# A hybrid encoder trunk on one core: the first norm's gain moved to the evictions, the later norms and the attention's last tiles moved into neighbouring products, and attention scores as two float32r products

## Chip, core and metric

The kernel runs on one core of a Trainium2 chip. The metric is device time in microseconds (us) of one execution, lower is better. Engines are named as in the profile: PE is TensorE's matrix products, PEld its weight loads, DVE is VectorE, ACT is ScalarE, POOL is GpSimd, SP is SyncE (which here only queues transfers).

## What is computed

Two layers over 512 tokens of width 1024, in float32. Cut to what matters here:

```python
def rms_norm(x, g):
    return x * lax.rsqrt(jnp.mean(x * x, axis=-1, keepdims=True) + EPS) * g

def fox_mix(h, w_in, fgate_b, q_g, k_g, w_out):       # 16 heads of 64
    q, k, v, fz = jnp.split(h @ w_in, [hd, 2 * hd, 3 * hd], axis=-1)
    q, k = rms_norm(q per head, q_g), rms_norm(k per head, k_g)
    c = jnp.cumsum(jax.nn.log_sigmoid(fz + fgate_b), axis=1)
    for each block i of 128 queries, keys :hi up to its end:
        logits = q[lo:hi] @ k[:hi].T * 64 ** -0.5 + c[lo:hi, None] - c[None, :hi]
        probs = softmax(where(causal, logits, -inf)); out = probs @ v[:hi]
    return concat(outs) @ w_out

def reference(x, ...):
    x = x + even_mix(rms_norm(x, g0))    # convolution and gated linear attention
    x = x + peer_ffn(rms_norm(x, g1))    # 16384 experts, 128 chosen per token
    x = x + fox_mix(rms_norm(x, g2))
    return x + peer_ffn(rms_norm(x, g3))
```

## The kernel before

One program runs four stages one after the other: `mix_even`, `peer(0)`, `mix_odd` and `peer(1)`. The residual `x` stays on the chip as four blocks of 128 tokens, `xb[0..3]`. Tile, the framework, gives each engine one fixed order of instructions (worked out when the program is built) and places the waits; the code sets it through the order in which it is written, through pools of buffers, and through `issue_after`.

Products of full precision are made of float32r pieces. `split` (L50 to 52) makes a high half on ACT (L51) and the rest on DVE or POOL (L52); `mm3` (L76 to 80) does high x high (L78), low x high (L79) and high x low (L80).

A norm (`rms_body`, L96) goes block by block. `scale` is a Square on ACT with the row's sum (L105), two small steps on DVE and POOL (L106, L107), and the scaling by the row's factor and the gain row `grow` on DVE (L108). `flip` transposes the block in two sets of four 128x128 squares on PE (L115) and evicts each set as `hhi` on ACT (L117) and `hlo` on DVE (L118). `grow` is the gain spread over 128 partitions by a load of 512 KB on SP (L86). `hhi` and `hlo` feed the projection behind the norm. A norm starts when the stage before it is through with `x`, and PE has the transposes to do and little else.

`mix_odd` is the attention. For each pair of heads, `project` makes 128 columns of q or k; `normalise` sums the squares on PE (L622), takes the root with Ln and Exp on ACT (L224, L225) and writes each head's 64 rows, scaled, to `qa` or `ka` (L628), whose two further rows are the cumulated gate and ones (queued on SP, L630). `logits` makes one score block (L640, float32, 66 rows deep) and adds the mask (L641); the softmax is L643 to L648; `flip` transposes the probabilities (L659), evicted to `PT` by ACT (L662) or DVE (L664); `values` multiplies them with v (L672). There are 64 units (head, block of queries); transposes of a unit follow three units after its scores. Units of one head pair lie between the projections of the next. The output projection `out_proj` (L195) follows when all units are done; it adds to `x` (L200).

`peer` begins with its norm, then runs expert steps `u_step` (L843, `pu` in the rows, 384 columns of blocks 1 to 3) and query projections; POOL gathers expert rows for block 0 by indirect transfers (L862, L873). It ends with `v_sweep`s (L1028), one per block, and the additions to `x` (L1062).

## Time and profile before

| | us |
|---|---|
| three runs, median (lowest to highest) | 3106.2 (3104.6 to 3106.36) |
| the profiled execution, its own time | 3103.41 |
| its span in the trace | 3101.6 |
| PE busy | 3058.7 (99%) |
| DVE, ACT, POOL busy | 2401.2, 1384.7, 1096.6 |
| `mix_even` / `peer(0)` / `mix_odd` / `peer(1)`, PE's first instruction of each at | 10 / 271 / 1530 / 1838 |

Busy time is an average over stages with different limits. PE's products are pipelined: a row's length exceeds the step from one to the next, so steps are read from the chain of waits or from the starts. A float32 product shows as two records. In the timeline, an entry in brackets is the idle time before the instruction and what ended it.

### The profile page before, as it was taken

How to read it: one execution, taken by the hardware profiler on the slowest of the kernel's cores; microseconds unless marked ns; L12 is line 12 of the kernel's file. 1: busy time of each engine (PE TensorE's matmuls, PEld its weight loads, DVE VectorE, ACT ScalarE, POOL GpSimd, SP SyncE). 2: the span in 40 equal slices, each digit the busy share in tenths (PEclk: the TensorE clock that was granted, in tenths of full speed). 3: DMA queues.
4: the chain of work that ended last, by engine and by line, in shares of the span. 5: the costliest groups of instructions: out<-in, count | busy, mean ns of one | idle time of the engine just before them, and what ended most of it. 6: DMA issues, size and time to landing. Idle time of an engine off the chain costs nothing.

```text
span 3101.6 us, 45719 instructions
## 1 busy us (share of the span) xinstructions
PE 3058.7 (99%) x15932; PEld 2684.7 (87%) x15932; DVE 2401.2 (77%) x4936; ACT 1384.7 (45%) x2224; POOL 1096.6 (35%) x800
## 2 busy tenths in 40 slices
PE   8999999999999999999999999999999999999999
PEld 6668999999999888888776679999999998888887
DVE  6764998888886888888645638898888867888886
ACT  4444334666664333333344523336666653333332
POOL 1220122976674222222100000227866752222220
PEclk9999999999999999999999999999999999999999
DMA  4113444999999899999421124448999998999996
GB/s 158 55 35 116 137 144 159 353 363 336 343 320 329 298 356 363 366 363 370 172 82 42 42 78 142 137 142 311 380 336 345 336 326 278 356 369 357 376 363 219
DMA packets 334201, 787.15 MB, mean 254 GB/s; under 512 B 26745, under 2 KB 181770, under 8 KB 327826
## 3 DMA queue, kind: packets, MB, share of 16 engines
q1 hardware_dynamic: 260242, 515.76, 47.5%
q0 software_dynamic: 73728, 268.47, 24.5%
q8 instruction: 125, 2.05, 0.3%
q14 instruction: 106, 0.87, 0.1%
HBM read 687.59 MB, written 96.47 MB: 253 GB/s over the span
## 4 chain that ended last, share of the span: by engine, by line
PE 92%; DVE 3%; issue 2%; DMA 1%; POOL 1%; ACT 1%; DVEq 0%; POOLq 0%; ACTq 0%
PE acc L1033 32%; PE pu L79 11%; PE pu L80 11%; PE pu L78 11%; PE bank L78 6%; PE bank L80 5%; PE bank L79 5%; PE bank L912 5%; PE pc L285 1%; PE po L672 1%; PE bank L640 1%; PE bank L936 1%; DMA gr<-in_uN_dram,ids 1%; DVE wlo L52 1%; PE bank L659 1%
## 5 line engine op out<-in xcount | busy, mean ns | idle before, releaser
L51 ACT ACTIVATE whi<-raw 128x1024 fp32r<-128x1024 f32 x604 | 639.8, 1060 | 1500.6 <-issue 584.8
L52 DVE TENSOR_TENSOR wlo<-raw,whi 128x1024 fp32r<-128x1024 f32 x565 | 692.4, 1226 | 339.1 <-ACT whi L51 309.7
L78 PE MATMUL pu<-hhi,whi 128*128 128x384 f32 x2048 | 699.1, 341 | 1.2 <-ACT hhi L117 1.2
L80 PE MATMUL pu<-hhi,wlo 128*128 128x384 f32 x2048 | 688.2, 336 | 2.6 <-DVE wlo L52 2.6
L79 PE MATMUL pu<-hlo,whi 128*128 128x384 f32 x2048 | 686.8, 335 | 0.0
L873 POOL DMA_INDIRECT gr<-in_vF_dram,ids x256 | 277.0, 1082 | 720.8 <-DVE x L875 696.2
L1033 PE MATMUL acc<-wlo,wh 128*128 128x512 f32 x1536 | 439.2, 389 | 0.0
L1033 PE MATMUL acc<-whi,wh 128*128 128x512 f32 x1536 | 439.1, 389 | 0.0
L862 POOL DMA_INDIRECT gr<-in_uN_dram,ids x256 | 349.2, 1364 | 252.4 <-DVE dots L864 157.3
L1033 PE MATMUL acc<-whi,wl 128*128 128x512 f32 x1536 | 436.8, 389 | 0.0
L78 PEld LDWEIGHTS pu<-hhi,whi 128*128 128x128 f32 x2048 | 386.2, 189 | 3.0 <-ACT hhi L117 1.7
L80 PEld LDWEIGHTS pu<-hhi,wlo 128*128 128x128 f32 x2048 | 385.6, 188 | 3.4 <-DVE wlo L52 3.2
L79 PEld LDWEIGHTS pu<-hlo,whi 128*128 128x128 f32 x2048 | 386.2, 189 | 1.7 <-DVE hlo L118 0.3
L1033 PEld LDWEIGHTS acc<-whi,wl 128*128 128x128 f32 x1536 | 288.4, 188 | 59.9
L1033 PEld LDWEIGHTS acc<-wlo,wh 128*128 128x128 f32 x1536 | 288.4, 188 | 59.7
L1033 PEld LDWEIGHTS acc<-whi,wh 128*128 128x128 f32 x1536 | 288.4, 188 | 59.5
L875 DVE SCALAR_TENSOR_TENSOR x<-gr,dots,x 128x1024 f32<-128x1024 f32 x256 | 327.2, 1278 | 0.0
L864 DVE CUSTOM_DVE_ANT_0 gr<-gr,h 128x1024 f32<-128x1024 f32 x256 | 308.6, 1225 | 20.9 <-DMA gr<-in_uN_dram,ids 20.7
L902 POOL TENSOR_SCALAR a<-cst,sT 128x128 f32<-128x128 f32 x192 | 316.3, 1648 | 15.2 <-PE bank L912 5.6
L52 POOL TENSOR_TENSOR wlo<-raw,whi 128x1024 fp32r<-128x1024 f32 x39 | 98.1, 2515 | 396.1 <-ACT whi L51 388.1
L899 DVE TENSOR_TENSOR a<-cst,sT 128x512 f32<-128x512 f32 x192 | 133.4, 695 | 126.2 <-PE bank L912 114.8
L78 PE MATMUL bank<-hhi,whi 128*128 128x512 f32 x512 | 211.5, 414 | 3.5 <-DVE hlo L118 2.7
(244 smaller groups left out, 4095.7 us busy)
## 6 DMA issues: line engine op xcount, KB each, us to landing
raw<-in_uT_dram SPq DMA_DIRECT2D x256, 512.0 KB
raw<-in_vF_dram SPq DMA_DIRECT2D x256, 512.0 KB
G<-big SPq DMA_DIRECT2D x48, 1024.0 KB
gc<-G SPq DMA_DIRECT2D x32, 1536.0 KB
aside<-xact SPq DMA_DIRECT2D x208, 192.0 KB
at<-aside SPq DMA_DIRECT2D x104, 384.0 KB
raw<-in_w_in_dram SPq DMA_DIRECT2D x32, 512.0 KB
raw<-in_wq_dram SPq DMA_DIRECT2D x32, 512.0 KB
```

Source lines behind the costliest of these rows:

```text
L51: first = self.nc.scalar.activation(hi, raw, AF.Copy)
L52: self.last_lo = (eng or self.nc.vector).tensor_tensor(lo, raw, hi.bitcast(F32), op=ALU.subtract)
L78: mm(out, lh, rh, start=first, stop=False)
L79: mm(out, lh, rl, start=False, stop=False)
L80: return mm(out, ll, rh, start=False, stop=last)
L862: nc.gpsimd.indirect_dma_start(out=r, out_offset=None, in_=uN, in_offset=bass.IndirectOffsetOnAxis(ap=ids[:, s:s + 1], axis=0))
L864: return lambda: nc.vector.tensor_tensor_reduce(r, r, h0, 1.0, 0.0, ALU.mult, ALU.add, accum_out=dots[:, s:s + 1])
L873: nc.gpsimd.indirect_dma_start(out=r, out_offset=None, in_=vF, in_offset=bass.IndirectOffsetOnAxis(ap=ids[:, s:s + 1], axis=0))
L875: return lambda: nc.vector.scalar_tensor_tensor(self.x0, r, dots[:, s:s + 1], self.x0, op0=ALU.mult, op1=ALU.add)
L902: (nc.vector if t else nc.gpsimd).tensor_scalar(a1[:, t], self.iota, e1[:, t:t + 1], gate[:, t:t + 1], op0=ALU.is_equal, op1=ALU.mult)
L912: nc.tensor.matmul(p[:, t], a2[:, t], a1[:, t], start=True, stop=True)
L1033: nc.tensor.matmul(acc[b][c], wt[:, s], vt[:, c], start=(n == 0 and wt is wh and vt is vh), stop=(n == NE1 - 1 and wt is wl))
```

## The change

1. **First norm** (`first_norm`). `scale` leaves the gain out; transposes go by columns, all four blocks of a column set into one bank, and the gain, now one number per partition (`gc0`), is applied by the eviction (`scale=` on ACT, and in the subtraction on DVE). The loads of x1 to x3 and of four weights stand at the head of SP's queue; the gain row of the next norm comes later. The conversion of `steps` moves to POOL, into `peer(0)`.
2. **Norms** (`norm`, in place of `rms_h`). Square writes its squares into the buffer that the scaled rows take. `scale` and `flip` can be called one by one. PEER 0's norm is called as before, with two buffers. The attention's norm is called in PEER 0's last `v_sweep`s, and its first value products (`start`) lie between its transposes. The norm of PEER 1 is called in the second half of `out_proj`. Block 0, the last, comes behind the first expert step.
3. **Scores**. `normalise` makes x scaled once for both heads (`xn`), splits it, and copies each high half to the other 64 partitions by transfers that POOL issues. Tile `a` holds (q: high, low; k: high, high), tile `b` (q: high; k: low) and four rows for the gate's sums and ones. A score is two float32r products, over `a` and `b`, of at least 256 columns. k has one pair of tiles now, q two. The gate's sums go through HBM (`cD`).
4. **Attention's end**. The last units run between the weights of `out_proj`'s first half. `values` is called before `flip`; `PT` has one buffer.

```diff
-        def scale(b):
...
             rs = self.np.tile([P, 1], F32, name="rs", bufs=NB)
-            xs[b] = h0 if b == 0 and h0 is not None else rp.tile([P, D], F32, name="xs", bufs=2)
-            sq = rp.tile([P, D], F32, name="sq")
-            self.last_sq = nc.scalar.activation(sq, self.xb[b], AF.Square, accum_out=ss)
+            xs[b] = rp.tile([P, D], F32, name="xs", bufs=blocks) if dst is None else dst
+            self.last_sq = nc.scalar.activation(xs[b], self.xb[b], AF.Square, accum_out=ss)
             nc.vector.tensor_scalar(ss, ss, 1.0 / D, EPS, op0=ALU.mult, op1=ALU.add)
             nc.gpsimd.tensor_tensor(rs, ss, self.mhalf, op=ALU.pow)
-            nc.vector.scalar_tensor_tensor(xs[b], self.xb[b], rs, self.grow, op0=ALU.mult, op1=ALU.mult)
...
     def mix_even(self):
         nc, tc, A = self.nc, self.tc, self.A
         hT = self.new_hT()
+        gc = self.np.tile([P, KD], F32, name="gc0")
+        nc.sync.dma_start(gc, A["gain0"])
+        for b in range(1, NB):
+            nc.sync.dma_start(self.xb[b], A["x"][b * P:(b + 1) * P])
+
+        self.early = [self.raw(A["w_in0"][i]) for i in (0, 4, 3, 7)]
         with tc.tile_pool(name="m0c", bufs=1) as sc:
-            self.rms_h(0, hT)
...
+            for k in range(KD):
+                p = self.bank([P, NB, P])
+                for b in range(NB):
+                    nc.tensor.transpose(p[:, b], xs[b][:, k * P:(k + 1) * P], self.ident)
+                p = p.rearrange("p b t -> p (b t)")
+                nc.scalar.activation(hT[0][:, k], p, AF.Copy, scale=gc[:, k:k + 1])
+                nc.vector.scalar_tensor_tensor(hT[1][:, k], p, gc[:, k:k + 1], hT[0][:, k].bitcast(F32),
+                                               op0=ALU.mult, op1=ALU.subtract)
```

The scores:

```diff
+                parts = [sb.tile([16, T], F32R, name=x, tag="t2", bufs=self.t2) for x in ("chi", "clo")]
+                self.split(pc, *parts)
+                for n, part in enumerate(parts):
+                    nc.sync.dma_start(cD[:, n], part.bitcast(F32))
...
             aug, PT, po = {}, {}, {}
-            qk = [[sp.tile([66, 2, T], F32, name=f"{x}a{j}") for j in range(2)] for x in "qk"]
+
+
+            qk = [[(sp.tile([P, 2, T], F32R, name=f"{x}a{j}"), sp.tile([68, 2, T], F32R, name=f"{x}b{j}"))
+                   for j in range(2 - w)] for w, x in enumerate("qk")]
...
+                for _, b in qk[w]:
+                    nc.gpsimd.dma_start(b[66 - 2 * w:68 - 2 * w], A["ends"][w])
...
-                a = qk[w][hp % 2]
+                a, b = qk[w][hp % len(qk[w])]
+                x = sb.tile([P, T], F32, name="xn", tag="t2", bufs=self.t2)
+                nc.vector.scalar_tensor_tensor(x, p, qkg[:, w:w + 1], rs, op0=ALU.mult, op1=ALU.mult)
                 for h in range(2):
-                    s = slice(h * 64, (h + 1) * 64)
-                    nc.vector.scalar_tensor_tensor(a[0:64, h], p[s], qkg[s, w:w + 1], rs[s],
-                                                   op0=ALU.mult, op1=ALU.mult)
-                    nc.sync.dma_start(a[64 + w:65 + w, h], cT[2 * hp + h:2 * hp + h + 1, w])
-                aug[hp, w] = a
+                    s, o = [slice(j * 64, (j + 1) * 64) for j in (h, 1 - h)]
+                    hi = a[s, h]
+                    nc.scalar.activation(hi, x[s], AF.Copy)
+                    lo, copy = (b[0:64, h], a[o, h]) if w else (a[o, h], b[0:64, h])
+                    nc.vector.tensor_tensor(lo, x[s], hi.bitcast(F32), op=ALU.subtract)
+                    nc.gpsimd.dma_start(copy, hi.bitcast(F32))
+                nc.gpsimd.dma_start(b[64 + 2 * w:66 + 2 * w], cD[2 * hp:2 * hp + 2].rearrange("h n t -> n h t"))
+                aug[hp, w] = a, b
...
                 pS = self.bank()
-                nc.tensor.matmul(pS[:, 0:n], qa[:, h, i * P:n], ka[:, h, 0:n], start=True, stop=False)
+                for j in range(2):
+                    nc.tensor.matmul(pS[:, 0:max(n, 2 * P)], aug[hp, 0][j][:, h, i * P:n],
+                                     aug[hp, 1][j][:, h, 0:max(n, 2 * P)], start=(j == 0), stop=False)
...
                 if i == 0:
-                    PT[hp, h] = sb.tile([P, NB, T], F32, name="PT")
+                    PT[hp, h] = sb.tile([P, NB, T], F32, name="PT", bufs=1)
...
+                if n - AHEAD - 1 >= 0 and units[n - AHEAD - 1][2] == NB - 1:
+                    values(*units[n - AHEAD - 1][:2])
                 if 0 <= n - AHEAD < len(units):
                     flip(units[n - AHEAD])
-                if n - AHEAD - 1 >= 0 and units[n - AHEAD - 1][2] == NB - 1:
-                    values(*units[n - AHEAD - 1][:2])
...
-            for _ in range(8 + AHEAD + 1):
-                unit()
-            self.out_proj(A["w_out1"], self.rows(oT))
+            self.hT = self.new_hT()
+            self.out_proj(A["w_out1"], self.rows(oT), i=3, hT=self.hT, between=lambda: [unit() for _ in range(4)],
+                          middle=lambda: pool.__exit__(None, None, None))
```

The projection's end, PEER's beginning and the last sweeps (`run` puts each call behind the one before in PE's order):

```diff
+        def ends(sweeps, acc):
+            run = self.chain()
+
+            def finish(b):
+                add(1, b, acc[b])
+                if b:
+                    nc.sync.dma_start(self.kept[b - 1], self.xb[b])
+                    scale(b)
+
+            for b in DB:
+                for f in sweeps:
+                    run(f, b)
+                finish(b)
+            for n, f in enumerate(sweeps):
+                if n == 0:
+                    run(flip, 1, hT)
+                    run(flip, 2, hT)
+                if n == 2:
+                    run(flip, 3, hT)
+                run(f, 0)
+            finish(0)
+            self.run = run
...
+            if L == 0:
+                nc.sync.dma_start(self.stf, A["steps"])
+                for w in range(2):
+                    nc.gpsimd.tensor_copy(self.steps[:, w], self.stf[:, w, :, None].to_broadcast([P, TOPK, TOPK]))
+                hT = self.new_hT()
+                self.keep()
+                scale, flip, close = self.norm(1, 2)
+                scale(1)
+                for b in DB:
+                    scale((b + 1) % NB, None if b < NB - 1 else h0)
+                    flip(b, hT)
+                    nc.sync.dma_start(self.kept[b - 1], self.xb[b])
+                run = lambda f, *args: f(*args)
...
+            def last():
+                run(flip, 0, hT)
+                close()
+                self.close_x()
...
+        run(lambda: u_step(0)[1])
+        nu = 1
+        last()
...
+        if L == 0:
+            hN, (scale, put, _), start = self.odd_begin()
+            with tc.issue_after(self.last_lo.ins):
+                scale(0)
+        run = self.chain()
         for b in range(nd):
-            v_sweep(tail, b)
+            run(v_sweep, tail, b)
             for c in range(2):
                 xa = self.xb[DB[b]][:, c * 512:(c + 1) * 512]
-                nc.vector.tensor_tensor(xa, xa, acc[b][c], op=ALU.add)
+                with tc.issue_after(self.last_xs.ins) if L == 0 else nullcontext():
+                    nc.vector.tensor_tensor(xa, xa, acc[b][c], op=ALU.add)
+            if L == 0:
+                scale(DB[b])
+                if b == 1:
+                    run(put, 0, hN, True)
+        if L == 0:
+            for b in DB:
+                run(put, b, hN, True)
+                run(start, b - 1)
+            run(start, NB - 1)
```

**SP's queue at the start.** `x` are the blocks of the input, `cst` constants, `stf` the steps, `raw` a weight as loaded. The queue before:

```order
1 L1076 DMA x_72<-in_x_dram 128x1024
2 L1077 DMA cst<-in_consts_dram 128x128
3 L1087 DMA stf<-in_steps_dram 128x32
4 L86 DMA grow<-in_gains_dram 128x1024
5 L1092 DMA x<-in_x_dram 128x1024 x3
6 L1093 DMA cst<-in_consts_dram 128x1024
7 L241 DMA cw<-in_conv_w_dram 128x124
8 L243 DMA ch<-in_conv_c_dram 128x12
```

SP's queue at the same place with the change:

```order
1 L1226 DMA x_72<-in_x_dram 128x1024
2 L1227 DMA cst<-in_consts_dram 128x128
3 L295 DMA gc_87<-in_gain_dram 128x8
4 L297 DMA x<-in_x_dram 128x1024 x3
5 L59 DMA raw<-in_w_in_dram 128x1024 x4
6 L301 DMA cst<-in_consts_dram 128x1024
7 L332 DMA cw<-in_conv_w_dram 128x124
8 L334 DMA ch<-in_conv_c_dram 128x12
9 L336 DMA gw_202<-in_gate_w_dram 17x256
10 L338 DMA glg<-in_gla_g_dram 128x1
11 L215 DMA wgr<-in_w_glr_dram 128x128
12 L95 DMA grow<-in_gains_dram 128x1024
```

The gain row went from ahead of x1 to x3 to the end of what is shown; four weights and the small `gc` came forward.

**PE and POOL in the attention**, where a unit of 512 columns and the sum of squares of the next pair stand. `idb` and `nmask` are the mask, `pr` the probabilities, `sq` the squares. PE there before:

```order
5722 L659 MATMUL bank<-cst,pr 128x128 x4
5723 L640 MATMUL bank<-ka_14268,qa_14266 128x512
5724 L641 LDWEIGHTS idb
5725 L641 MATMUL bank<-nmask,idb 128x128
5726 L672 MATMUL po<-PT,v 64x512
5727 L672 MATMUL po<-PT,v 64x384
5728 L672 MATMUL po<-PT,v 64x256
5729 L672 MATMUL po<-PT,v 64x128
5730 L659 MATMUL bank<-cst,pr 128x128
5731 L622 MATMUL bank<-sq,cst 128x512
```

PE at the same place now; the score is two rows, and the values kept their place behind it:

```order
5755 L776 MATMUL bank<-cst,pr 128x128 x4
5756 L756 MATMUL bank<-ka_14265,qa_14263 128x512
5757 L756 MATMUL bank<-kb_14266,qb_14264 128x512
5758 L758 LDWEIGHTS idb
5759 L758 MATMUL bank<-nmask,idb 128x128
5760 L789 MATMUL po<-PT,v 64x512
5761 L789 MATMUL po<-PT,v 64x384
5762 L789 MATMUL po<-PT,v 64x256
5763 L789 MATMUL po<-PT,v 64x128
5764 L776 MATMUL bank<-cst,pr 128x128
5765 L733 MATMUL bank<-sq,cst 128x512
5766 L87 MATMUL bank<-hhi,whi 128x512
```

POOL now, from its first three loads of the rows of sums on (before, POOL has no instruction among the attention's units):

```order
224 L746 DMA qb_14262<-cD 2x2x512
225 L746 DMA kb_14266<-cD 2x2x512
226 L746 DMA qb_14264<-cD 2x2x512
227 L745 DMA qb_14262<-qa_14261 64x512 x2
228 L745 DMA ka_14265<-ka_14265 64x512 x2
229 L745 DMA qb_14264<-qa_14263 64x512 x2
230 L746 DMA kb_14266<-cD 2x2x512
231 L746 DMA qb_14262<-cD 2x2x512
```

On POOL the copies stand in the order in which the pairs are normalised, each behind the loads of the sums.

**PE at the norm ahead of PEER 1.** `o` is the attention's output, `h` of the last block's rows `h_...` the scaled block 0, `pu` the first expert step. PE there before:

```order
6279 L79 MATMUL bank<-wlo,ohi 128x512
6280 L80 MATMUL bank<-whi,olo 128x512
6281 L115 MATMUL bank<-cst,xs 128x128 x24
6282 L78 MATMUL pu<-hhi,whi 128x384
6283 L115 MATMUL bank<-cst,h_16386 128x128 x8
6284 L78 MATMUL bank<-hhi,whi 128x512 x2
6285 L79 MATMUL pu<-hlo,whi 128x384
6286 L80 MATMUL pu<-hhi,wlo 128x384
```

PE now, from the transposes of block 3 to the first expert step:

```order
6341 L89 MATMUL bank<-whi,olo 128x512
6342 L120 MATMUL bank<-cst,xs 128x128 x8
6343 L87 MATMUL bank<-whi,ohi 128x512
6344 L88 MATMUL bank<-wlo,ohi 128x512
6345 L89 MATMUL bank<-whi,olo 128x512
6346 L87 MATMUL bank<-whi,ohi 128x512
6347 L88 MATMUL bank<-wlo,ohi 128x512
6348 L89 MATMUL bank<-whi,olo 128x512
6349 L87 MATMUL pu<-hhi,whi 128x384
6350 L88 MATMUL pu<-hlo,whi 128x384
```

The transposes of blocks 1 and 2 (16, not shown) and of block 3 (x8) now have products of the projection's second half behind them, twelve and six; block 0's eight moved behind the 24 products of the first expert step.

## Rows read from the trace of the kernel before

**Rows 1.** The page, part 1: busy us (share of the span) and instructions of each engine.
```profile
PE 3058.7 (99%) x15932; PEld 2684.7 (87%) x15932; DVE 2401.2 (77%) x4936; ACT 1384.7 (45%) x2224; POOL 1096.6 (35%) x800
```

**Rows 2.** Timeline of the start: start, length (us), engine, line, operation, [idle before <-releaser].
```profile
0.73 0.39 SPq L1076 DMA_DIRECT2D x<-in_x_dram  x1
...
4.42 1.06 ACT L105 ACTIVATE sq<-x 128x1024 f32<-128x1024 f32 x1 [2.42 <-DMA x<-in_x_dram]
...
8.94 0.36 SPq L247 DMA_DIRECT2D glg<-in_gla_g_dram  x1
9.06 1.29 DVE L108 SCALAR_TENSOR_TENSOR xs<-x,rs,grow 128x1024 f32<-128x1024 f32 x1 [3.30 <-DMA grow<-in_gains_dram]
10.23 0.33 SPq L189 DMA_DIRECT2D wgr<-in_w_glr_dram  x1
...
16.54 1.28 DVE L108 SCALAR_TENSOR_TENSOR xs<-x,rs,grow 128x1024 f32<-128x1024 f32 x1 [0.44 <-POOL rs L107]
```

**Rows 3.** Windows: from:to, length, busy us of PE, PEld, DVE, ACT, POOL; PEclk granted.
```profile
24.62:29.60 4.98, 4.97 (x12) 3.96 (x13) 1.68 (x2) 0.00 (x0) 0.00 (x0) 0.52 0.69 211
271.42:287.39 15.97, 11.39 (x58) 9.81 (x57) 11.51 (x15) 7.88 (x13) 0.55 (x1) 0.79 0.40 132
1835.61:1854.90 19.29, 12.87 (x58) 11.57 (x59) 14.19 (x20) 8.32 (x13) 3.21 (x4) 0.73 0.25 82
```

**Rows 4.** Chain of waits: start, length, what; a set of transposes, then float32r products.
```profile
1776.58 0.44 PE bank L659 x4
...
1854.73 0.17 PE pu L79
1854.90 0.23 PE bank L79
```

**Rows 5.** Timeline of PE, 1526 to 1546: the two rows with a wait.
```profile
1532.53 0.50 PE L78 MATMUL bank<-whi,hhi 128*128 128x512 f32 x1 [1.52 <-ACT hhi L117]
...
1538.93 1.06 PE L115 MATMUL bank<-cst,xs 128*128 128x128 f32 x8 [1.83 <-DVE xs L108]
```

**Rows 6.** Chain of waits in the attention: float32 scores of 256, 384, 512 and 128 columns.
```profile
1775.05 0.43 PE bank L640 x2
...
1775.87 0.65 PE bank L640 x2
...
1777.02 0.86 PE bank L640 x2
...
1778.05 0.22 PE bank L640 x2
```

**Rows 7.** Timeline of the attention, 1767 to 1776: a key normalise and the values.
```profile
1770.36 0.60 ACT L662 ACTIVATE PT<-bank 128x512 f32<-128x512 f32 x1
...
1770.58 1.02 PE L622 MATMUL bank<-sq,cst 128*128 128x512 f32 x2
...
1771.54 2.37 PE L672 MATMUL po<-PT,v 128*64 128x512 f32 x8
...
1772.09 0.68 ACT L224 ACTIVATE rs<-bank,sc 128x512 f32<-128x512 f32 x1
...
1772.80 0.63 ACT L225 ACTIVATE rs<-rs 128x512 f32<-128x512 f32 x1
```

**Rows 8.** Timelines of POOL and of DVE, 530 to 575: gathers of 512 KB.
```profile
535.66 2.17 POOL L862 DMA_INDIRECT gr<-in_uN_dram,ids  x1 [27.64 <-DVE ids L945]
...
541.12 0.94 POOL L862 DMA_INDIRECT gr<-in_uN_dram,ids  x1 [0.30 <-issue]
...
561.05 1.93 POOL L862 DMA_INDIRECT gr<-in_uN_dram,ids  x1 [0.17 <-DVE a L902]
...
535.56 1.23 DVE L52 TENSOR_TENSOR wlo<-raw,whi 128x1024 fp32r<-128x1024 f32 x1 [0.20 <-ACT whi L51]
...
542.77 1.49 DVE L864 CUSTOM_DVE_ANT_0 gr<-gr,h 128x1024 f32<-128x1024 f32 x1 [2.51 <-DMA gr<-in_uN_dram,ids]
...
569.60 1.22 DVE L864 CUSTOM_DVE_ANT_0 gr<-gr,h 128x1024 f32<-128x1024 f32 x1 [2.83 <-DMA gr<-in_uN_dram,ids]
```

More of the change, by code (lines that the diff above doesn't have):

```diff
@@ L128, in new_hT, with chain, run @@
+    def chain(self):
+        last = []
+        def run(f, *args):
+            if last:
+                with self.tc.issue_after(last.pop().ins):
+                    last.append(f(*args))
+            else:
+                last.append(f(*args))
+            return last[0]
+        return run
     def new_hT(self):
@@ L178, in rest @@
                 ws = load(order[end:])
[L179 to L181 removed]
+                done([lambda b, w=w: sweep([w], [b]) for w in ws], acc)
             return acc
@@ L200, in add, with plain @@
             nc.vector.tensor_tensor(xa, xa, acc, op=ALU.add)
-        for b, acc in enumerate(self.proj_nat(w[0], yT, order=order)):
-            add(0, b, acc)
-        self.proj_nat(w[1], yT, order=order, done=lambda b, acc: add(1, b, acc))
+        def ends(sweeps, acc):
[18 more added lines that the diff above has]
+            self.run = run
+        def plain(sweeps, acc):
+            for b in BLOCKS:
+                for f in sweeps:
+                    f(b)
+                add(1, b, acc[b])
+        for b, acc in enumerate(self.proj_nat(w[0], yT, order=order, between=between)):
+            add(0, b, acc)
+        if middle:
+            middle()
+        if i is not None:
+            self.keep()
+            self.next_norm = scale, flip, _ = self.norm(i)
+        self.proj_nat(w[1], yT, order=order, done=plain if i is None else ends)
     def log_sigmoid(self, sp, z, shape, dst):
```

176 lines of the change are left out of this document (100 added, 76 removed).

## The prediction

> **What bounds the kernel now.** The page comes first: PE is busy for 3058.7 of 3101.6 us, 99% [rows 1]. So a us goes only where PE's own instructions get shorter, or where one of its few waits or slow-clock stretches closes. The other engines matter through what they make PE wait for. I then cut the places where PE is not dense into stretches (the windows view), read the start in the timeline, took PE's steps from the chain of waits, and read the chain of the attention's normalise and the only transfers that POOL issues now.
>
> The reader should see this. At the start x0's Square begins at 4.42, but the scaling waits for the gain row until 9.06; and the last scaling begins at 16.54 [rows 2]. From 24.62 to 29.60 PE is busy throughout, 4.97 of 4.98, at a granted clock of 0.52 [rows 3]; from 24.62 on it has no holes. That clock is the lower of its two levels (1.2 of 2.4 GHz), after a stretch in which PE had often waited. The norm ahead of each PEER has the same shape: 15.97 and 19.29 us at a clock of 0.79 and 0.73 [rows 3].
>
> **The parts, and what each costs.**
>
> *First norm.* The gain row leaves the head of SP's queue. Its 512 KB land just before 9.06; small loads behind it are released at 8.94 and 10.23, so 512 KB take 1.29 us [rows 2]. Without it x1 to x3 can land at 4.42 + 1.29, 2.58 and 3.87 = 8.3. Square (1.06) and scaling (1.29) [rows 2], with some 1.2 for the two small steps between, put the last scaled block at 11.8, against 17.8 before. Transposes, evictions (eight copies and eight subtractions in both kernels) and the first weight's low half take about 2.5 more: dense products from 14.3. The kernel before had done four products, 0.9, before its 24.62. Gain 24.6 - 14.3 - 0.9 = 9.4, less 0.9 for two weight subtractions that DVE does between the eight blocks: **-8.5**. Ends: -4.5, the 4.6 from 4.42 to 9.06 in which the gain row landed and no more, and -10.5, without those 0.9 and with the weight's low half early. The slow clock after it stays as long as now.
>
> *Norm ahead of PEER 0.* The window of 15.97 holds 32 transposes, 24 products of 384 columns and two of 512. At full steps (0.11, a quarter of the 0.44 of four; 0.17; 0.23 [rows 4]) that is 8.1, so 7.9 are lost [rows 3]. The change keeps two buffers for scaled rows, but Square now writes into them, so block 3's Square waits for block 1's transposes and, on ACT, for two evictions. From the order this delays its scaling by about 2.8, and block 0's likewise; the first expert step, already behind block 0, is dense 1 to 2 us later: **+2** (0 to +4).
>
> *Norm ahead of the attention.* Its blocks' transposes now stand between the last expert sweeps and the first value products. PE waited 1.52 and 1.83 there [rows 5]; each now has 12 products (2.8) or a sweep ahead of it: **-3.4** (-2 to -3.7).
>
> *Scores.* Per four units the float32 product takes 0.22, 0.43, 0.65 and 0.86 [rows 6]; the 16 sets sum to 34.6. The new one is two float32r products of at least 256 columns. Those of 384 and 512 have rows: 0.17 and 0.23 [rows 4]. For 256 there is none: between 0.11 (half of 512) and 0.17; I take 0.12, since 0.17 to 0.23 grows with the columns. Per set 2 x (0.12 + 0.12 + 0.17 + 0.23) = 1.28, times 16 = 20.5: **-14.1** (-10.9 with 0.17 for 256).
>
> *The normalise that feeds them.* Before, two 64-row scalings on DVE ended it. Now one 128-row scaling (an estimate of 0.75, a little over half of the 1.29 for 1024 columns [rows 2]), then a copy of each head's high half on ACT (0.6, as the PT eviction of 512 columns [rows 7]), a subtraction, and a copy of that half to the other 64 partitions, which POOL issues. From the start of the sum of squares: about 0.9 for it, 0.6 more where an exponential stands before it on ACT, 0.68 and 0.63 for Ln and Exp [rows 7], 0.75, 0.6: 4.3. PE's cover up to the first score that reads the copy: 24 products and the values, 8.7, for six head pairs, and 6.4 for the first two. So a transfer has 4.35 us free of charge, or 2.6 and 2.05. A plain copy that POOL issues has no row. Nearest in size and solitude is the load of x0, 512 KB in an empty queue: queued at 0.73, used at 4.42 [rows 2], 3.7; less three quarters of 1.29 for 128 KB, 2.7. POOL's issue costs 0.94 to 2.17 [rows 8], I take 1.4: 4.1 in all. The six pairs then wait for nothing, the first two 1.5 and 2.05: +3.6. The upper end is the first gather, 7.1 from issue to use [rows 8], and at 512 KB: 6 x 2.75 + 4.5 + 5.05 = +26; the lower end, 0.94 + 2.7, gives +2.6. POOL does nothing else in the attention; queued behind a late copy are the next pair's rows of sums and copies, whose readers are 20 us away. The first pair's four scores, 0.9 shorter in all, cover less of its first softmax: +0.9. Together **+4.5**.
>
> The issue of 0.94 at 541.12 lies within the 2.51 in which DVE idled before 542.77, that of 2.17 beside a subtraction on DVE [rows 8]. The Trainium skill's page "DMA: Bandwidth & Descriptors", section "SWDGE vs HWDGE vs iDMA", says why that may be: the descriptors that GpSimd writes lie in SBUF, out of which DVE locks it in its two-port mode, and transfers from SP are immune. By that rule, with DVE at work on every copy, at 2.17 + 2.7 a copy, the copies' term would be +8.2 instead of +3.6, and without it +2.6; the sum moves by 4.6 up or 1 down. The same page's fit (2.0 us plus bytes over 436e3 per us) gives about 2.3 for 128 KB, an estimate by which the sum would be 3.3 lower.
>
> *Values.* They stand behind the 512-column score in both kernels. PT's eviction began at 1770.36, took 0.60, and the values began at 1771.54 [rows 7]; the cover falls by 0.4: **+1** (0 to +2.5).
>
> *Norm ahead of PEER 1.* The window of 19.29 holds the same 8.1 of work, so 11.2 are lost [rows 3, 4]. The blocks' transposes now lie in the projection's second half. Blocks 1 and 2 have 18 or more products in front, enough. Block 3's chain (add, Square, scaling, some 4.4) meets 16 transposes and 12 products (4.5), but its low halves come late: some 1.5. Block 0's has only the first expert step, 24 x 0.17 = 4.1, and starts behind block 3's subtractions: 0.9. Its evictions then queue on ACT behind three weight copies of 128x1024, each as long as Square's 1.06 [rows 2], and an activation: 2.4. The projection's third weight waits behind four additions on DVE: 1.3. Of 11.2 some 6 stay: **-5** (-2 to -9).
>
> The rest of the PEERs, 2800 us, changes in buffers alone; the wait for the experts' loads is not touched. The steps' conversion on POOL (two casts) and 32 fewer small loads on SP lie beside PE: nothing; were they not covered, under 1.
>
> Sum: -8.5 + 2 - 3.4 - 14.1 + 4.5 + 1 - 5 = **-23.5**. The profiled execution took 3103.4 and would take 3079.9; the median shown is 3106.2, 2.8 above it, and becomes **3083**.
>
> **Rivals.**
>
> 1. *The copies are late in every head pair* (slower). If a copy takes X, the waits are 6(X - 4.35) + (X - 2.6) + (X - 2.05) = 8X - 30.8. The other terms make -27.1, so it decides from X = 7.2. The first gather's 7.1 is there; the tenth, issued at 561.05 and used at 569.60, took 8.5 [rows 8], which makes 37 - 27 = +10: 3116. Against it: those carry 512 KB each among loads that fill the queues. The rule on locked descriptors (the Trainium skill's page "DMA: Bandwidth & Descriptors", section "SWDGE vs HWDGE vs iDMA") would lead there if it held landing up too. Chance 0.08.
>
> 2. *The holes close only to open elsewhere*: at the start, -4.5; PEER 0's norm +4; the two others 0, PE waiting on ACT or DVE in the new order. With scores, normalise and values: -4.5 + 4 - 14.1 + 4.5 + 1 = -9.1, 3097. For it: these chains lie on ACT, DVE and POOL and got no shorter. Against: 18 products cover most of one. Chance 0.12.
>
> 3. *The change does not make the scores as short*: a float32r product below 512 columns costs what 512 cost. 8 x 0.23 x 16 = 29.4, so -5.1 instead of -14.1: 3092. Against: 384 columns take 0.17 [rows 4]. Chance 0.05.
>
> **The numbers.** The forecast has 0.75. Its own ends, not all at once: 3070 (start -10.5, last norm -9, normalise +2.6) to 3096. Range: 3070 to 3098, which takes in rivals 2 and 3 at their values and leaves out rival 1 and the tails. 0.2%, 6.2 us, is what a measurement can tell: faster means under 3100. All of rivals 2 and 3 but a tail, and nearly all of the forecast: faster 0.88; same 0.05; slower 0.07.
>
> **What would show it.** Right: dense products from about 14; the score's pieces 0.23 to 0.46 per unit; no PE wait on a POOL transfer from the third head pair on; the two last norms' windows without long waits, the clock at 1.0; a PE wait of 1 to 3 us on ACT behind block 0's transposes in PEER 1. Wrong: waits of over 2 us ahead of the first score in each head pair (rival 1); windows about the norms as long as now, or a clock of 0.5 in the attention (2); 256-column pieces at 0.23 (3); or other steps in the experts' sweeps, for which I allow nothing.

## The result, and the profile after

The changed kernel takes 3128.7 us (median of four runs, 3127.4 to 3130.1) against 3106.0 (3104.6 to 3106.4) for the kernel before beside it: a ratio of 1.0072, with a 95% interval of 1.0059 to 1.0085. It is slower by 22.8 us. The ratios of the experiments further down are taken in the same way, against runs of the kernel before beside them, with the interval in brackets. The forecast was 3083, with a range to 3098.

The page of the changed kernel, part 1, which answers to [rows 1], and two of the groups of part 5 (line, engine, operation, names, shapes, count | busy, mean ns of one | idle before):

```profile
PE 3079.3 (98%) x15932; PEld 2679.1 (86%) x15932; DVE 2412.1 (77%) x4953; ACT 1404.9 (45%) x2255; POOL 1137.6 (36%) x851
...
L1166 PE MATMUL acc<-whi,wh 128*128 128x512 f32 x1536 | 450.9, 396 | 0.0
L1166 PE MATMUL acc<-wlo,wh 128*128 128x512 f32 x1536 | 450.7, 396 | 0.0
```

PE has as many instructions as before and is 20.6 us longer at work. The L1166 groups are the value sweeps, in which each expert's values stream past the gated activations (4608 products of 512 columns in the two PEERs). The kernel before has them at 389 ns each. A duration there is from start to modelled end; what counts is how often one starts. Windows of 400 us within the sweeps of PEER 0 and PEER 1 show that (from:to, length, busy us of PE and of PEld with their counts, granted clock, the DMA engines' share and GB/s). The kernel before, then the changed one:

```profile
1100.00:1500.00 400.00, 400.00 (x1766) 331.35 (x1765) 1.00 1.01 359
2600.00:3000.00 400.00, 400.00 (x1767) 331.31 (x1766) 1.00 1.01 359
```

```profile
1100.00:1500.00 400.00, 400.00 (x1716) 322.00 (x1715) 1.00 1.00 351
2600.00:3000.00 400.00, 400.00 (x1716) 322.03 (x1715) 1.00 0.99 346
```

Both are full, with no wait and the clock at 1.0. From the starts of the single products, one begins every 226.7 ns before and every 233.3 after. Times 4608 that is 30.6 us, more than the whole loss.

Stations of PE along the span, in us from its start, put the rest in its place:

| station | before | after | difference | change of it |
|---|---|---|---|---|
| first transposes of PEER 0's norm | 271.26 | 264.89 | -6.4 | -6.4 |
| first gate product, PEER 0 | 544.99 | 537.91 | -7.1 | -0.7 |
| first value sweep, PEER 0 | 1003.49 | 998.38 | -5.1 | +2.0 |
| last product of that sweep | 1529.75 | 1541.11 | +11.4 | **+16.5** |
| first sum of squares, attention | 1578.68 | 1588.19 | +9.5 | -1.9 |
| first gate product, PEER 1 | 2111.84 | 2119.75 | +7.9 | **-1.6** |
| first value sweep, PEER 1 | 2570.25 | 2580.66 | +10.4 | +2.5 |
| last product of that sweep | 3096.51 | 3122.20 | +25.7 | **+15.3** |

So there are two questions. Why do the sweeps' products start at longer steps, though the change touches neither them nor their data? And why did the stretch from the attention to PEER 1's gates, for which -13.6 was forecast (scores, normalise, values, norm), bring only -1.6?

### The profile page after: what moved, and what is told of

The parts are those of the page before. It is cut to its first block, busy times and chain, and to the rows that moved or that the text cites. A ratio compares the mean times of both kernels' runs of the same rounds, so it can differ in the third digit from the quotient of the medians.

```text
span 3127.7 us, 45800 instructions
## 1 busy us (share of the span) xinstructions
PE 3079.3 (98%) x15932; PEld 2679.1 (86%) x15932; DVE 2412.1 (77%) x4953; ACT 1404.9 (45%) x2255; POOL 1137.6 (36%) x851
## 4 chain that ended last, share of the span: by engine, by line
PE 89%; DVE 3%; DMA 3%; ACT 2%; issue 1%; POOL 1%; SPq 0%; DVEq 0%; POOLq 0%; ACTq 0%
PE acc L1166 34%; PE pu L87 10%; PE pu L89 10%; PE pu L88 10%; PE bank L87 5%; PE bank L88 5%; PE bank L89 5%; PE bank L1040 5%; DMA gr<-in_uN_dram,ids 2%; PE po L789 1%; PE pc L376 1%; PE bank L1068 1%; DVE wlo L54 1%; ACT whi L53 1%; PE bank L467 0%
## 5 line engine op out<-in xcount | busy, mean ns | idle before, releaser
L1166 PE MATMUL acc<-whi,wh 128*128 128x512 f32 x1536 | 450.9, 396 | 0.0
L1166 PE MATMUL acc<-wlo,wh 128*128 128x512 f32 x1536 | 450.7, 396 | 0.0
L1166 PE MATMUL acc<-whi,wl 128*128 128x512 f32 x1536 | 449.4, 395 | 0.0
L990 POOL DMA_INDIRECT gr<-in_uN_dram,ids x256 | 340.8, 1331 | 237.7 <-DVE dots L992 140.8
L1030 POOL TENSOR_SCALAR a<-cst,sT 128x128 f32<-128x128 f32 x192 | 345.2, 1799 | 14.0 <-PE bank L1040 8.0
L1166 PEld LDWEIGHTS acc<-whi,wl 128*128 128x128 f32 x1536 | 288.5, 188 | 69.8
L1166 PEld LDWEIGHTS acc<-wlo,wh 128*128 128x128 f32 x1536 | 288.5, 188 | 69.7
L1166 PEld LDWEIGHTS acc<-whi,wh 128*128 128x128 f32 x1536 | 288.4, 188 | 69.6
L992 DVE CUSTOM_DVE_ANT_0 gr<-gr,h 128x1024 f32<-128x1024 f32 x256 | 308.2, 1222 | 25.7 <-DMA gr<-in_uN_dram,ids 25.4
```

Of the source, the lines that this page charges most:

```text
L990: nc.gpsimd.indirect_dma_start(out=r, out_offset=None, in_=uN, in_offset=bass.IndirectOffsetOnAxis(ap=ids[:, s:s + 1], axis=0))
L992: return lambda: nc.vector.tensor_tensor_reduce(r, r, h0, 1.0, 0.0, ALU.mult, ALU.add, accum_out=dots[:, s:s + 1])
L1030: (nc.vector if t else nc.gpsimd).tensor_scalar(a1[:, t], self.iota, e1[:, t:t + 1], gate[:, t:t + 1], op0=ALU.is_equal, op1=ALU.mult)
L1166: mm = nc.tensor.matmul(acc[b][c], wt[:, s], vt[:, c], start=(n == 0 and wt is wh and vt is vh), stop=(n == NE1 - 1 and wt is wl))
```

## Experiments: the sweeps

What the change does do there is to move tiles. The program's allocation lists the addresses within a partition: the moving operand, the expert's values in whi and wlo, stands where it stood, from 42784. The sweep's weight tiles wh and wl went from 188448 to 163904, into the new pool pw. First theory: the place matters. A probe and two variants test it.

**Place, by itself.** The probe's core:

```
for m, f, wo, vo in ((MOVING[0], even, 0, 0), (MOVING[1], even, 0, 0), (MOVING[2], even, 0, 0),
                     (MOVING[0], odd, 8, 8), (MOVING[0], mixed, 0, 8)):
    vt = [[R[m][:, vo + k * 1008 + c * 512:vo + k * 1008 + (c + 1) * 512] for c in range(2)]
          for k in range(2)]
    for t in R:
        wh, wl = t[:, wo:wo + 384], t[:, wo + 384:wo + 768]
        ...
```

`R` are the 24 tiles; `MOVING` are those at 48, 112 and 176 KB; 8 floats are 32 bytes.

> A probe that computes nothing of the reference: it fills SBUF with 24 tiles of 8 KB, named by the kilobyte of a partition at which each begins (at24k to at208k), and then runs products of 128x512 in float32r alone, in the pattern of the value sweep (three weight sets, two halves, three blocks of rows, 36 per pair of places): the weights stand in each of the 24 tiles in turn, the moving operand at 48 KB, then at 112 KB, then at 176 KB; then at 48 KB again with both operands 32 bytes further, and with the moving operand alone 32 bytes further. No other engine and no DMA works meanwhile. Theory (the place of the weights in SBUF sets the step of a product): with the moving operand at 48 KB, weights at about 120 to 168 KB step every 233 ns, weights at 40 to 96 KB and from 184 KB every 227 ns; the 32 bytes change nothing. First rival (the offset within 64 bytes sets it, since the weights moved from 32 to 0): every place steps at one pace, and the runs with 32 bytes differ from those without by 6 ns. Second rival (other engines' or DMA traffic near the weights slows the reads): 227 ns at every place, as nothing else runs here.

Windows of the probe, 36 products each, weights at 160 KB: moving operand at 48, 112 and 176 KB, then both 32 bytes further, then the moving operand alone 32 bytes further.

```profile
152.26:160.58 8.32, 8.32 (x38) 6.77 (x36) 0.00 (x0) 0.00 (x0) 0.00 (x0) 1.00 0.00 0
351.94:360.26 8.32, 8.32 (x38) 6.77 (x36) 0.00 (x0) 0.00 (x0) 0.00 (x0) 1.00 0.01 2
551.62:559.94 8.32, 8.32 (x38) 6.77 (x36) 0.00 (x0) 0.00 (x0) 0.00 (x0) 1.00 0.00 0
751.30:759.62 8.32, 8.32 (x37) 6.76 (x36) 0.00 (x0) 0.00 (x0) 0.00 (x0) 1.00 0.00 0
952.34:960.74 8.40, 8.40 (x37) 6.76 (x36) 0.00 (x0) 0.00 (x0) 0.00 (x0) 1.00 0.00 0
```

The place makes no difference: 231.1 ns (8.32 / 36) at every one of the 24 places, but for the very first pair, at the start, where the granted clock was still at the lower level. Only the last window differs, 233.3 ns. What changed in it is the offset between the operands. (The 231.1 is itself a mixture: a third of the products take their moving operand from the second half, `k` of 1, 4032 bytes further, which is 192 bytes off modulo 256.)

**Other places in the changed kernel, and the new pool in the kernel before.**

```diff
-gcs[m] = vb.tile([P, NTG, EC * TG], F32, name="gc")
+gcs[m] = (wb if L else vb).tile([P, NTG, EC * TG], F32, name="gc", bufs=2)
...
-ats[n] = vb.tile([P, 2, TD], F32, name="at", bufs=3)
+ats[n] = (vb if L else ab).tile([P, 2, TD], F32, name="at", bufs=3)
...
+apool = tc.tile_pool(name=f"pa{L}", bufs=3, reuse_waits="tile")
...
-wb, vb = wpool.__enter__(), vpool.__enter__()
+ab, wb, vb = apool.__enter__(), wpool.__enter__(), vpool.__enter__()
```

> The changed kernel with the value sweep's weight tiles wh and wl moved to other places in SBUF, nothing else: in the first PEER from 160 to 169 KB of the partition (the act tiles' ring goes below them), in the second to 184 KB, where they stood before the change (the gate rows' ring goes below them). Theory (place): the second PEER's 2304 products step at 226.7 ns again instead of 233.3, 15 us less; the first PEER's place, 169 to 178 KB, lies between the slow and the fast ones known, so 233 or 227: 3113.5 us with the first still slow, 3098.5 with both fast. Rival (the change of code around the sweep, its own pool or the order of its engines, and not the place): 3128 to 3130 us, steps 233 in both.

Measured: 3129.7 us, 1.0072 [1.0056, 1.0089]; the windows have 1716 products again in both PEERs. The second PEER's tiles were back at 184 KB, at 188480, and no faster.

```diff
-wh = vb.tile([P, TD], F32R, name="wh", bufs=3)
-wl = vb.tile([P, TD], F32R, name="wl", bufs=3)
+wh = wb.tile([P, TD], F32R, name="wh")
+wl = wb.tile([P, TD], F32R, name="wl")
...
+wpool = tc.tile_pool(name=f"pw{L}", bufs=3, reuse_waits="tile")
...
```

> The kernel before with this one piece of the change alone: wh and wl in a pool of their own that opens ahead of the value sweep's other pool, which puts them at 160 KB of the partition instead of 184 KB. The orders of TensorE, VectorE, ScalarE and GpSimd stay those of before, instruction for instruction. Theory (place): 4608 products at 233.3 instead of 226.7 ns, 30.6 us more, 3136.5 us (3133 to 3139). Rival (the step is slow for another part of the change): 3105 to 3107 us.

Measured: 3106.5 us, 1.000 [0.9991, 1.001]; its window in PEER 0:

```profile
1100.00:1500.00 400.00, 400.00 (x1767) 331.20 (x1766) 1.00 1.01 359
```

The place theory falls twice: tiles at their old place are slow, tiles at the new place (163872 here) are fast. But 188480 is 32 bytes beyond the old 188448, and 163872 is 32 bytes short of the changed kernel's 163904. Those 32 bytes come from one tile: the column of gains gc0, 8 floats, which is allocated behind the moving operand's tiles and ahead of the sweep's weights.

**The offset.** The next runs take the 32 bytes apart. The second probe runs every pair of eight offsets (`STEP` is 32):

```
W = [filled(f"w{STEP * i}b", 1024 + 8) for i in range(8)]
M = [filled(f"m{STEP * i}b", 2048 + 8) for i in range(8)]
...
for w in W:
    for m in M:
        sweep(w, m)
```

> A probe that computes nothing of the reference: the products of the first probe again, in the pattern of the value sweep, between eight weight tiles and eight moving tiles whose addresses within a partition step by 32 bytes (w0b to w224b, m0b to m224b, counted from a common multiple of 128), 36 products for each of the 64 pairs; then four weight tiles against m0b shifted by 4, 8 and 16 bytes. Theory (the step depends on the two operands' offset from each other modulo 128 bytes, whatever the place): 226.7 ns where the two names differ by 0 or 128 bytes, 233.3 ns for every other pair, and for the shifts of 4, 8 and 16 bytes as well. First rival (modulo 64): 226.7 ns also where the names differ by 64 or 192. Second rival (modulo 256): 233.3 ns where they differ by 128. Third rival (the first probe's 231 and 233 ns came from its own pattern): one pace for all 64.

Its windows for w0b with m0b, m32b, ... m224b, 36 products each:

```profile
31.81:39.97 8.16, 8.16 (x37) 1.00 0.01 2
39.97:48.38 8.41, 8.41 (x38) 1.00 0.00 0
48.38:56.63 8.25, 8.25 (x38) 1.00 0.00 0
56.63:65.04 8.41, 8.41 (x37) 1.00 0.01 2
65.04:73.44 8.40, 8.40 (x38) 1.00 0.00 0
73.44:81.87 8.43, 8.43 (x38) 1.00 0.00 0
81.87:90.27 8.40, 8.40 (x38) 1.00 0.00 0
90.27:98.66 8.39, 8.39 (x37) 1.00 0.01 2
```

Equal offsets give 226.7 ns (8.16 / 36); a moving operand 64 bytes ahead 229.2; the others 233 to 234. The other seven rows of the grid repeat this, shifted, within 1 ns, so only the difference counts. It counts modulo 256: m0b with w192b, 192 bytes behind, has 228.8 as 64 ahead has, and at a difference of 128 the step is as slow as at 32. My theory had said modulo 128, so the second rival was right. Shifts of 4, 8 and 16 bytes are slow as well (230 to 240 ns).

**One tile's size.** First the changed kernel with nothing but one tile made larger, then the kernel before with nothing but one small tile added; each engine's instructions stay in the same order:

```diff
-gc = self.np.tile([P, KD], F32, name="gc0")
+gc = self.np.tile([P, 32], F32, name="gc0")[:, 0:KD]
```

> The changed kernel with one tile made larger, nothing else, each engine's instructions in the same order: the new column of gains gc0 takes 128 bytes of a partition instead of 32, so that everything allocated behind it stands 96 bytes further, with its offset modulo 128 what it was before the change. Theory (the 32 bytes of gc0 put the sweep's weights 32 bytes off the moving operand's line): the 4608 products step at 226.7 ns again, 30.6 us less; and if the gate products' GpSimd instructions (1799 ns each instead of 1648) come of the same offset, 4 us more: 3091 to 3099 us, faster than the kernel before. Rival (the pool of its own or something else in the change, not the offset): 3127 to 3131 us.

Measured: 3124.6 us, 1.0050 [1.0037, 1.0063], 1723 products in each window:

```profile
1100.00:1500.00 400.00, 400.00 (x1723) 324.30 (x1722) 1.00 0.99 351
```

A miss that fits the probe: the weights are now at 164000, 128 away from the moving operand modulo 256, at 232.4 ns instead of 226.7.

```diff
+self.np.tile([P, KD], F32, name="gc0")
 self.load_gain(first)
```

> The kernel before with one unused tile of 32 bytes in the pool of the norms, nothing else, each engine's instructions in the same order: everything allocated behind it stands 32 bytes further. Theory (offset): 4608 products at 233.3 instead of 226.7 ns, 30.6 us more, and up to 4 us more in the gate products: 3135 to 3143 us. Rival (the offset does nothing by itself): 3105 to 3108 us.

Measured: 3137.2 us, 1.0092 [1.0079, 1.0105]. An unused tile of 32 bytes costs the kernel before 29.3 us; its windows:

```profile
1100.00:1500.00 400.00, 400.00 (x1716) 322.01 (x1715) 0.00 (x0) 1.00 1.00 352
2600.00:3000.00 400.00, 400.00 (x1716) 322.03 (x1715) 0.00 (x0) 1.00 0.99 343
```

Then the changed kernel with 64 floats, 256 bytes, in the same tile:

> The changed kernel with one tile made larger, nothing else, each engine's instructions in the same order: the gain column gc0 takes 256 bytes, so that everything behind it stands where it stood modulo 256 before the change. Theory (the step depends on the two operands' offset modulo 256, as the second probe shows; the run with 128 bytes put them 128 apart and so stayed slow): all 4608 products of the value sweeps at 226.7 ns, 30.6 us less than the changed kernel: 3094 to 3100 us, faster than the kernel before. Rival (the pool of its own for the sweep's weights has a part in it): 3120 us or more.

Measured: **3096.9 us**, 0.9969 [0.9958, 0.9981], and its windows:

```profile
1100.00:1500.00 400.00, 400.00 (x1767) 331.20 (x1766) 1.00 1.01 360
2600.00:3000.00 400.00, 400.00 (x1766) 331.22 (x1765) 1.00 1.02 360
```

This settles it. The address offset, set by one tile of 32 bytes, is the 30.6 us; without it the change is faster than the kernel before.

| kernel | weights at, modulo 256 | moving, modulo 256 | ns per product |
|---|---|---|---|
| before | 188448, 32 | 32 | 226.7 |
| after | 163904, 64 | 32 | 233.3 |
| other places | 173120 and 188480, 64 | 32 | 233.3 |
| before, own pool | 163872, 32 | 32 | 226.7 |
| gain of 128 bytes | 164000, 160 | 32 | 232.4 |
| before, 32 bytes | 188480, 64 | 32 | 233.3 |
| gain of 256 bytes | 164128, 32 | 32 | 226.7 |

## Experiments: the attention

From one query projection's sum of squares to the next is one head pair. Windows of a pair (busy us of PE, PEld, DVE, ACT, POOL, then the granted clock), of the kernel before and of the changed one:

```profile
1711.16:1735.90 24.74, 24.74 (x114) 16.59 (x113) 15.00 (x37) 11.74 (x28) 0.00 (x0) 1.00 0.14 43
```

```profile
1697.65:1722.72 25.07, 23.42 (x113) 16.22 (x113) 16.11 (x39) 14.04 (x32) 3.23 (x6) 1.00 0.24 64
```

PE's work shrank by 1.32, the scores, and 1.65 of idle time opened. The waits view of PE from 1588 to 1860 names it (engine, what, us in total, times, longest):

```profile
PE bank L733 <- ACT sq L726: 6.2, 6, 1.0
PE po L789 <- DVE PT L781: 3.0, 5, 0.6
PE bank L756 <- ACT PT L779: 1.5, 2, 0.8
PE bank L776 <- DVE pr L765: 1.2, 1, 1.2
```

Before, the same view (1578 to 1848) has 2.4 us on the attention's own products; now it has 15.7. The lines of before:

```profile
PE bank L659 <- DVE pr L648: 1.4, 1, 1.4
PE bank L659 <- DVE den L647: 0.6, 1, 0.6
PE bank L640 <- issue: 0.4, 1, 0.4
```

In a pair of the changed kernel it is 1.04 ahead of the sum of squares and 0.61 ahead of the values. The chain of waits through such a pair, its end:

```profile
1680.73 0.03 ACT pr L763
1680.76 0.45 issue
1681.21 0.19 ACT pr L763
1681.40 0.95 ACT whi L53
1682.35 0.50 ACT sq L726
1682.84 0.04 issue
1682.89 1.12 PE bank L733 x2
```

From 1675.6 to the sum of squares this chain has no piece on PE: it runs over xn, the copies of the high halves, the subtractions, the softmax, whi and sq, on ACT and DVE. In the kernel before the chain lies on PE throughout such a stretch (1666 to 1678). The squares sit on ACT behind whi, the high half of weights that are due three projections later.

The granted clock took some 1.8 us besides (20 x 0.09, an estimate): it was 0.91 from 1612 to 1632, and 1.00 in the attention of the kernel before. In the 10 us ahead of the fall PE was busy for 8.56, in the kernel before at the same place for 8.58, so the traces do not show why it fell.

```diff
-p = self.proj_T(wi[8 * w + hp], hT, between=between)
+p = self.proj_T(wi[8 * w + hp], hT, between=between, after=sqs[-3] if len(sqs) > 4 else None)
...
-nc.scalar.activation(sq, p, AF.Square)
+sqs.append(nc.scalar.activation(sq, p, AF.Square))
```

> The changed kernel with one order changed on ScalarE: in the attention each projection's squares (sq) go ahead of the copy whi of the weights that are due three projections later and that take the place that the same projection has just left. Theory (the shorter scores only uncovered waits on ScalarE and VectorE: TensorE waits 6.2 us for sq behind whi and 3.0 us for the probabilities' copy PT behind wlo): both waits go, 6 to 9 us less, 3120 to 3123 us. Rival (the two engines are the bound of a head pair, and the wait only moves to the next consumer): 3127 to 3130 us, the same sum of TensorE's waits in the attention under other names.

Measured: 3124.9 us, 1.0063 [1.0046, 1.008], which the times alone do not tell from the changed kernel's 1.0072. In the trace the stretch from the first sum of squares to PEER 1's first expert step goes from 265.9 to 262.0 us. The wait for sq falls from 6.2 to 1.3, the values' wait of 3.0 for PT on DVE goes, and the later pairs take some 24.2 instead of 25.07; other waits come up (2.1 for pr, 1.3 of the values for PT on ACT, and one of 1.0 of a score for a copy). Theory and rival share it: about 4 of the 9 us.

Then two parts undone, on the base with the gain column of 256 bytes, where the sweeps no longer hide what the attention does. First the scores (of the edit, the product alone):

```diff
-for j in range(2):
-    nc.tensor.matmul(pS[:, 0:max(n, 2 * P)], aug[hp, 0][j][:, h, i * P:n],
-                     aug[hp, 1][j][:, h, 0:max(n, 2 * P)], start=(j == 0), stop=False)
+nc.tensor.matmul(pS[:, 0:n], qa[:, h, i * P:n], ka[:, h, 0:n], start=True, stop=False)
```

> The run with the gain column of 256 bytes, with one part of the change undone: the attention's scores are again one float32 product of 66 rows, with the operands written and augmented as before the change; the rest of the change stands. Theory (the shorter scores gave their 10.4 us back to waits on ScalarE and VectorE which they uncovered): undoing them lengthens the score products by 10.4 us and takes away most of the 10 us of waits in the head pairs, so the time stays within 3 us of the run with 256 bytes. Rival (the score part is worth its 10 us, and the waits come from the values that now run ahead of the flips, with one buffer for PT): 7 to 11 us more than the run with 256 bytes.

Measured: 3096.5 us, 0.9964 [0.9951, 0.9978], against 3096.9: by the times the shorter scores are worth nothing that can be told. The later pairs are back at 24.74, and PE does not wait in them. In the trace the stretch from the first sum of squares to PEER 1's first expert step is 4.4 us longer than with the short scores. The same columns as above, with the float32 scores, then on the base:

```profile
1572.81:1841.61 268.80, 263.92 (x1162) 182.57 (x1161) 145.22 (x324) 110.76 (x238) 1.66 (x3) 0.98 0.17 54
1575.57:1839.99 264.42, 248.53 (x1162) 177.71 (x1161) 152.18 (x339) 129.99 (x271) 27.58 (x51) 1.00 0.25 71
```

With float32 scores PE is 15.4 us longer at work and idles 11.0 less: what the short scores save comes back as idle time. The granted clock accounts for the 4.4: it was 0.91 from 1600 to 1620 and 0.86 from 1790 to 1815, and 1.00 in both on the base, which makes 5.3 us (20 x 0.09 + 25 x 0.14, an estimate). In the 10 us ahead of the second fall PE was busy for 8.27 in both kernels, so why it fell in one of them is not shown. PEER 0's gate phase, from its first gate product to its first value sweep, was 4.3 shorter instead, 458.5 against 462.8; of these 1.6 are again the clock, 0.91 from 612 to 630 on the base. Over all the traces a gate phase took 458.4 to 460.5 us without the change and 458.5 to 462.9 with it. The +2.0 and +2.5 of the stations lie within that; their cause stays open.

```diff
-PT[hp, h] = sb.tile([P, NB, T], F32, name="PT", bufs=1)
+PT[hp, h] = sb.tile([P, NB, T], F32, name="PT")
...
```

In the part not shown the values go behind the flips again; the run starts from the last kernel of this section.

> The run with squares and line, with the other part of the attention's change undone: the transposed probabilities PT have two buffers again and the values run behind the flips (one of six half-kilobyte work tiles is given up for the room). Theory (the single buffer with the values ahead of the flips makes TensorE wait for PT, 3.0 us in five waits of the changed kernel): those waits go, 1 to 3 us less than the run with squares and line. Rival (the wait only moves to the flips behind): the same time within 1 us.

Measured: 3096.5 us, 0.9964 [0.995, 0.9978]: not faster than its base (3094.1), and the waits for PT on ACT are still there, 1.6. The rival holds. (The work tile given up is 2 KB of a partition, not half a kilobyte.)

**Together.** The squares first, the gain column larger, and a gap ahead of oT, the attention's output. First with the gain of 128 bytes, forecast before that gain's own run had missed:

> The changed kernel with the gain column of 128 bytes, with the squares ahead of the weight copies in the attention as in the run before, and with 64 bytes left free ahead of the attention's output oT, so that the output projection's weights stand on the moving operand's line too. Theory: the time of the run with the gain column of 128 bytes, less 3.9 us for the squares, less 192 x 6.7 ns = 1.3 us for the projection: 3086 to 3094 us. Rival (the squares' gain was a chance of that run's order): no faster than the run with the gain column alone, less 1.3 us.

Measured: 3121.4 us, 1.0039 [1.0026, 1.0052]; like its base it was 128 bytes off. Then with 256, and oT put on the moving operand's offset modulo 256:

> The run with the gain column of 256 bytes, with the attention's squares ahead of the weight copies on ScalarE, and with 192 bytes left free ahead of oT, which puts the output projection's weights on the moving operand's offset modulo 256 as well. Theory: 3.9 us less for the squares and 192 x 6.6 ns = 1.3 us less for the projection than the run with 256 bytes: 3089 to 3095 us. Rival (the two do nothing on this base): the time of the run with 256 bytes.

Measured: **3094.1 us**, 0.9959 [0.9946, 0.9973], the best of all kernels here, some 13 us faster than the kernel before. The trace has the attention's stretch 3.1 us shorter than with the gain column alone, and the output projection's products at 227 instead of 234 ns (medians of their steps); by the times the two kernels are not told apart.

## Why the prediction was wrong

**The step that failed** is the one after the sum's terms: "The rest of the PEERs, 2800 us, changes in buffers alone; the wait for the experts' loads is not touched", which I put at nothing without comparing where the tiles stand before and after. The change in buffers cost 30.6 us in the two sweeps, by the offset of the weights from the moving operand: a product every 233.3 ns instead of 226.7. (PEER 0's sweeps took 1.2 more, because eight transposes of the next norm, some 0.9, now stand between the last of them.) The text's last sentence of what would make it wrong, "other steps in the experts' sweeps", is what the trace showed. No rival had it; the one that ended slower, late copies, was not it.

With the offset mended (3096.9) the forecast's sign is right and its size is not: 9.6 us are gained by the ratio, not 23.5. By its terms:

- *First norm, -8.5.* PE reached the next norm 6.4 earlier. Dense products start at 18.69, not 14.3. The slow clock did not stay as long as before, as I had assumed: in the 4.98 us from there the granted clock was 0.83, against 0.52 [rows 3], which gave back some 1.5 (4.98 x 0.31, an estimate). The miss shows in the start's timeline:

```profile
12.41 2.87 POOL L54 TENSOR_TENSOR wlo<-raw,whi 128x1024 fp32r<-128x1024 f32 x1
13.64 2.72 DVE L54 TENSOR_TENSOR wlo<-raw,whi 128x1024 fp32r<-128x1024 f32 x1 [0.57 <-ACT whi L53]
...
17.07 1.33 PE L322 MATMUL bank<-cst,xs 128*128 128x128 f32 x5 [2.89 <-DVE hlo L325]
```

  A subtraction that DVE does in 1.23 elsewhere [rows 8] took 2.72 beside POOL's 2.87, ahead of the first low halves, and PE waited 2.89 for those.
- *Norm ahead of PEER 0, +2.* One wait for the scaling came, 3.0, as argued; others went, and the stretch to the gates is 0.7 shorter.
- *Norm ahead of the attention, -3.4.* Measured -1.9 behind the sweeps, -0.7 with the 1.2 that its transposes added to them. Two waits for the scaled rows are left, 2.4 in all, though each block now has products ahead of it.
- *Scores, -14.1.* PE's steps through the scores sum to 24.6 us instead of 35.0: -10.4. The columns stepped near the 0.12, 0.17 and 0.23 assumed only in the second product of a score (0.13 and 0.18, and 0.24 for 512, waits aside); the first took 0.16, 0.22 and 0.32.
- *Normalise, +4.5.* The mechanism was wrong. I counted on a chain of 4.3 us plus a copy of 4.1. Copies cost nothing here: none of PE's waits is on one. The list of DMA issues has them at 2.4 us from issue to landing:

```profile
ka<-ka POOLq DMA_DIRECT2D x16, 128.0 KB, 2.4
```

  What I did not count is what the shorter scores and the longer normalise do to the order on ACT and DVE: sq behind whi, PT behind wlo. That is 13 us of new waits, against +5.5 for normalise and values together. This was the kind of wait that rival 2 named for the norms and that I did not look for here: I compared PE's cover with one chain, the copies', and not with the next one on the same engines.
- *Norm ahead of PEER 1, -5.* Within its ends (-2 to -9), and better than -5: from 1826 to 1880 PE's waits sum to 3.0 and the clock stays at 1.0, so of 11.2 some 3 stay and not 6. The window as long as the one of [rows 3], about the first expert step:

```profile
1846.40:1865.70 19.30, 17.10 (x99) 14.69 (x98) 14.29 (x19) 11.92 (x18) 1.10 (x2) 1.00 0.39 128
```

  PE is busy for 17.10 instead of 12.87, the clock is at 1.00 instead of 0.73, and the wait of 1.5 on ACT behind block 0's transposes, for which I had 2.4, is there.

The Trainium skill's page "DMA: Bandwidth & Descriptors", section "Anatomy of one DMA — SWDGE (gpsimd) path", has a fit by which a copy of 128 KB takes an estimated 2.3 us; the trace's 2.4 agrees. The same page of the Trainium skill, section "SWDGE vs HWDGE vs iDMA", says that DVE in its two-port mode locks GpSimd out of the SBUF state into which it writes a transfer's descriptors; that does not show in these copies: POOL's issues of them took 0.53 us on average, while DVE was at work for 16.1 of a pair's 25.1 us. How much of that work was in the two-port mode the trace does not say.

## What to carry to other kernels

A change that allocates anything moves everything allocated behind it. Before calling a stage untouched, compare the addresses of the two operands of its products before and after; here 32 bytes cost 31 us, and padding the tile to 256 bytes gave them back. And where a faster instruction uncovers two other engines, follow the chain on those engines to the next thing that PE reads, not only the one new operand: the scores' 10 us were worth nothing in the times, because the pair's chain had moved from PE to ACT and DVE.

## What the chip showed unexpectedly

With every other engine idle and the granted clock at 1.0, products of 128x512 in float32r, each with its own weight load, start every 226.7 ns when the moving operand and the weights have the same address modulo 256, every 229 when the moving operand is 64 bytes ahead, and every 232 to 234 at the other multiples of 32 (second probe). The whole kernels agree: 226.7 at the same address modulo 256, 233.3 at 32 bytes off, 232.4 at 128. The place itself made no difference at the 24 places tried (first probe). The Trainium skill's page "SBUF — State Buffer", section "A bandwidth-pool intuition that's wrong (but worth ruling out)", gives weight loads a second, independent read port, by which one would not expect the offset between the two to matter; the second probe's 8.16 and 8.41 us differ from that, and decide. What in the chip makes the difference no run here shows.
